# Reordering the latent attention heads of a one-layer block: maxima two items ahead, an earlier shift and row, earlier value products

## The chip, the cores and the metric

The kernel runs on one core of one Trainium2 chip. The metric is the device time of one execution in microseconds (us). The profile is of one profiled execution of the same program; its times count from the start of its span.

## What is computed

The reference is one layer over 1024 latent tokens and 256 context tokens of width 1024, in float32: a half-step SwiGLU, then two token mixers on one normalised input (neighbourhood attention and multi-head latent attention), gated, merged and projected, then a second half-step SwiGLU. The change touches the latent attention: 8 heads, 96 channels for queries and keys (64 plain, 32 rotary), 64 for values; every latent query attends to all 1280 keys.

```python
def _attend(q, k, v):
    s = jnp.einsum('bqhd,bkhd->bhqk', q * q.shape[-1] ** -0.5, k).astype(jnp.float32)
    p = jax.nn.softmax(s, axis=-1).astype(v.dtype)
    return jnp.einsum('bhqk,bkhd->bqhd', p, v)
...
        k_mla = jnp.concatenate([k_ctx_mla, _mla_k(kn, _axial_rope(kr, ang_r, ang_c))], axis=1)
        v_mla = jnp.concatenate([cvb, vb], axis=1)
        o_mla = _blocked_attention(q_mla, k_mla, v_mla)
```

## The kernel before

All matrix products that need float32 accuracy are done as three matmuls of a high and a low part (high x high, high x low, low x high). The layer is a chain of stages: first SwiGLU, projections, neighbourhood attention (`NaItem`, 32 items), latent attention (`MlaItem`, 16 items), merge, second SwiGLU.

A latent item is one head and half of the queries (512); items 2h and 2h+1 belong to head h. The scores are kept with keys on the partitions and queries along the free axis, in ten blocks of 128 keys. These are its steps, with the lines and the names that the profile shows:

- `maxima()` (from L1938): ten steps. Each is a matmul of high parts alone, queries on the partitions, into an `m` bank (bm), and a maximum along it on VectorE (DVE, L1944). The sixteen items have 160 such steps in all; the generator `tops` chains those of all items in order, and each `next(tops)` does one.
- `shift()` (L1963 to L1965): three small DVE operations that turn the maxima into the negated maximum of each query (n_).
- `row()`: a PE transpose of n_ (bm<-ident,st on L160), a DVE copy of it to `kr` (L1972), and four DMAs of 0.5 KB (w<-kr) that write it as row 96 of the head's query tile `qh`. The key tile has ones in that row, so the first score matmul, with 97 rows, subtracts the maximum.
- `scores(kb)`: three matmuls into an `s` bank (bs<-w,w), then the exponential on ScalarE (ACT, L1985). What the text calls block kb is this call with what the loop does behind it.
- `add(kb)`: the sums for the denominator, blocks 0 to 6 on GpSimd (POOL, L1996 and L1998), 7 to 9 on DVE (L2001, L2003); `total()` (L2006) joins both on DVE.
- `weigh()`, the value products: 40 matmuls into a `v` bank (bv<-xp,w) and four of ones with the total (bv<-t,strip) for the denominator.
- `out()`: reciprocal (L2020) and product (L2021) on DVE, a copy on ACT (L1757), and in `heads_out` four output steps on POOL (L1760, L1761).

`MlaHead.first()` issues ten DMAs that load a head's high queries, high keys, context keys and low queries (w<-d); the first four of them bring the high queries and the high latent keys, which the first maximum reads. It also sets the rows of ones with two memsets on POOL. `second()` issues three, for the low keys and the values.

What sets the order of the work: the loop at L2185 calls, for each item and block, `scores`, one or more steps of `tops`, and `follow(i, kb)`, in which the other steps of the preceding item (`prev`), the item itself and the next one (`after`) are written out by block. Matmuls, transposes and DMA issues are pinned to the order of the source (`pin` in L157, L160, L135; all DMAs go through SyncE's queue, SP). DVE, ACT and POOL operations of this stage are not pinned; their order is chosen at build time. Three `m` banks, three `s` banks, two `v` banks, 16 weight tiles `w` and four exponential tiles `xp` (two an item) are shared in turn.

Ahead of the loop the last three neighbourhood items (n = 29, 30, 31) do steps of `tops` in place of scores ahead; the last of them calls `mla_heads[1].first()`, `mla[0].shift()` and, behind its first part, `mla[0].row()`. After the loop `follow(16, kb)` ends the last item, between steps of `FirstMerge` (matmuls bs<-xo,w of the next stage).

Of the kernel before, what the change touches and what calls it, by code (L numbers as in the profile page):

```python
# [22 lines left out]
NH = 8  # L23
# [20 lines left out]
def hybrid_block(ctx: ExitStack, tc: tile.TileContext, a: dict, out: bass.AP):  # L44
# [1230 lines left out]
    def emit_cq(i, ci, x, bank):  # L1275

        t, q = x, T2()
        if bank:
            t = T2()
            act.copy(t, x)  # L1280
        act.activation(q, t, AF.Square)
        if ci in sq:
            vec.tensor_tensor(sq[ci], sq[ci], q, op=ALU.add)
        else:
            sq[ci] = q
        store(cqx[i, :, ci * 512:(ci + 1) * 512], t)
# [22 lines left out]
    for p in range(3):  # L1309
        punits.append(Unit(h2, [cq_src(2 * p), cq_src(2 * p + 1)],  # L1310
                           lambda i, ci, x, bank, p=p: emit_cq(2 * p + i, ci, x, bank)))
# [619 lines left out]
    class MlaItem:  # L1931
# [55 lines left out]
        def part(self, kb):  # L1987
            return self.pt[kb // 5][:, (kb % 5) * 512:(kb % 5) * 512 + 512]
# [39 lines left out]
    soft, started, todo, pending = [], [], [], []  # L2028
    AHEAD, LAG, EARLY = 3, 2, 2

    def start(n):

        if n < len(todo):
            it = todo[n]()
            started.append(it)
            yield from it.scores()
# [79 lines left out]
    tops = chain(*[x.maxima() for x in mla])  # L2116

    def top(n):
        for _ in range(n):
            next(tops, None)  # L2120
            yield
# [3 lines left out]
    def finish_one():  # L2125
        if ending:
            ending.pop(0)()

    for n in range(len(todo)):
        if n == len(todo) - 4:  # L2130
            mla_heads[0].first()
        if n == len(todo) - 2:
            mla_heads[0].second()
        if n == len(todo) - 1:
            mla_heads[1].first()
            mla[0].shift()
        ahead = chain(start(EARLY), start(AHEAD)) if n == 0 else start(n + AHEAD) if n + AHEAD < len(todo) else top(5)
        parts = led_parts[n] if n in led_parts else started[n].values()
        many = len(parts)
        soft_n = list(soft)  # L2140
        for x, part in enumerate(parts):
            pending.append(part() or [])
            take = -(-len(soft_n) // (many - x))
            for f in soft_n[:take]:
                soft.remove(f)
                f()
            del soft_n[:take]
            for _ in range(3 if n == 0 else 1 if n + AHEAD < len(todo) else 2):
                next(ahead, None)
            finish_one()  # L2150
            if len(pending) > LAG:
                ending += pending.pop(0)
                finish_one()
            if n == len(todo) - 1 and x == 0:
                mla[0].row()
        if n == 0:
            next(na1)
        for _ in ahead:
            pass

    def follow(i, kb):


        prev = mla[i - 1] if i else None
        item = mla[i] if i < len(mla) else None
        after = mla[i + 1] if i + 1 < len(mla) else None
        if kb == 0 and prev:
            prev.add(9)
            prev.total()
        if kb == 0 and i % 2 == 0 and i // 2 + 1 < NH:  # L2170
            mla_heads[i // 2 + 1].second()
        if kb == 3 and prev:
            prev.weigh()
        if kb == 4 and prev:
            prev.out()
        if item and kb > 1:
            item.add(kb - 1)
        if after and kb == 5:
            after.shift()
        if kb == 5 and i % 2 and i // 2 + 2 < NH:  # L2180
            mla_heads[i // 2 + 2].first()
        if after and kb == 6:
            after.row()

    for i, item in enumerate(mla):  # L2185
        for kb in range(10):
            item.scores(kb)
            next(tops, None)
            if i == 0:
                finish_one()  # L2190
                if pending and kb % 2 == 0:
                    ending += pending.pop(0)
            follow(i, kb)
            if i >= 14 and kb == 0:
                fm.load(i - 14)
            if i >= 14 and kb == 5:
                fm.split()
    for kb in range(5):
        follow(len(mla), kb)
        for _ in range(3 if kb < 2 else 2):  # L2200
            if fm.left:
                fm.step()
# [264 lines left out]
```

## Time and profile before

| | before |
|---|---|
| median of 3 runs | 2584.81 us (2584.32 to 2588.14) |
| profiled execution | 2584.02 us |
| its span | 2582.2 us |
| PE busy | 2513.7 us (97%) |
| DVE busy | 1853.8 us (72%) |
| ACT busy | 1124.1 us (44%) |
| POOL busy | 301.0 us (12%) |

PE is TensorE. The profile has several views: the page of the whole execution, the waits (who waited for whom, total, times, longest), the instructions in order of time (start, duration, engine, line, operation, output<-input, count, and in brackets the idle time before it and what ended it), the busy time of each engine in stretches (with the granted TensorE clock as a share of full speed), the groups by line, and the DMA issues with the time to landing. L157 is the helper that issues every matmul, L160 every transpose, L135 every DMA, so these are told apart by the tiles that they name. The latent attention lies between 1471 and 1775 us of the span.

### The profile page before, as it was taken

Reading aid. Unit: us, or ns where it says so; the run is one execution under the profiler, and the core shown is the slowest. Engines: PE = TensorE matmul, PEld = TensorE weight load, DVE = VectorE, ACT = ScalarE, POOL = GpSimd, SP = SyncE. Lnnn points to the kernel's source line nnn. Section 1 sums busy time; section 2 is a strip of 40 time slices with the busy share of each in tenths; the row PEclk is TensorE's granted clock in tenths of the full one; section 3 lists DMA queues with packets and bytes.
Section 4 is the critical chain, followed back from the end, with each engine's and each line's share of the span. In section 5 each row is a group of like instructions: output and inputs, shape, how many; then the busy total and the mean of one; then the engine's idle time right before and its main releaser. Section 6 shows DMA issues by size and latency. Waiting matters only on the chain.

```text
span 2582.2 us, 36926 instructions
## 1 busy us (share of the span) xinstructions
PE 2513.7 (97%) x13176; PEld 2080.6 (81%) x13176; DVE 1853.8 (72%) x3162; ACT 1124.1 (44%) x2007; POOL 301.0 (12%) x400
## 2 busy tenths in 40 slices
PE   8999999999999999999999988889999999999998
PEld 6888888888998888889888766667888888888887
DVE  4789986797676588863457666655886888767777
ACT  6623223446654743433538533332267322323444
POOL 1000000001100000001003465553011000000003
PEclk9999999999999999999999999889999999999999
DMA  8555543943674666765857422205846444326824
GB/s 305 164 171 193 190 152 125 342 135 124 236 265 151 236 219 203 261 214 119 285 209 262 126 66 55 62 20 191 315 143 230 151 162 163 115 102 226 280 70 163
DMA packets 247673, 464.74 MB, mean 180 GB/s; under 512 B 61057, under 2 KB 77633, under 8 KB 247489
## 3 DMA queue, kind: packets, MB, share of 16 engines
q1 hardware_dynamic: 247488, 462.38, 53.9%
q8 instruction: 104, 1.70, 0.3%
q14 instruction: 81, 0.66, 0.1%
HBM read 341.59 MB, written 120.65 MB: 179 GB/s over the span
## 4 chain that ended last, share of the span: by engine, by line
PE 90%; DVE 4%; ACT 2%; DMA 2%; issue 1%; SPq 1%; POOL 0%; DVEq 0%; POOLq 0%; ACTq 0%
PE bs L157 38%; PE bm L157 28%; PE bv L157 21%; PE bm L160 2%; DVE t L2020 1%; DVE st L1944 1%; PE bs L160 1%; ACT t L123 1%; SPq L135 1%; DMA w<-kr 1%; DVE xu L123 0%; ACT xu L123 0%; DVE st L1964 0%; ACT xv L123 0%; PE bv L160 0%
## 5 line engine op out<-in xcount | busy, mean ns | idle before, releaser
L123 ACT CAST xu<-t 128x512 fp32r<-128x512 f32 (+1 forms) x270 | 161.0, 601 | 493.7 <-DVE t L123 352.4
L157 PE MATMUL bm<-xu,xu 128*128 128x512 f32 (+2 forms) x1572 | 366.6, 386 | 0.0
L157 PE MATMUL bs<-xv,xu 128*128 128x512 f32 x1488 | 357.4, 389 | 0.3 <-DVE t L123 0.3
L157 PE MATMUL bv<-xv,xu 128*128 128x512 f32 x1342 | 335.4, 389 | 0.0
L157 PEld LDWEIGHTS bm<-xu,xu 128*128 128x128 f32 x1572 | 288.0, 188 | 56.8 <-ACT t L123 0.2
L157 PEld LDWEIGHTS bs<-xv,xu 128*128 128x128 f32 x1488 | 279.1, 188 | 59.0 <-issue 1.1
L157 PEld LDWEIGHTS bv<-xv,xu 128*128 128x128 f32 x1342 | 251.8, 188 | 52.2
L157 PE MATMUL bs<-xv,xv 128*128 128x512 f32 x1086 | 265.9, 390 | 0.0
L123 DVE TENSOR_TENSOR xu<-xu,xu 128x512 fp32r<-128x512 f32 (+1 forms) x296 | 201.8, 686 | 74.4 <-ACT xu L123 74.1
L123 POOL TENSOR_SCALAR st<-st 128x1 f32<-128x1 f32 (+1 forms) x66 | 33.6, 510 | 1882.3 <-ACT t L123 1864.1
L157 PEld LDWEIGHTS bs<-xv,xv 128*128 128x128 f32 x1086 | 203.0, 188 | 41.7
L157 PE MATMUL bs<-w,w 96*128 96x512 f32 (+1 forms) x736 | 210.7, 405 | 16.3 <-DMA w<-kr 13.6
L157 PE MATMUL bs<-xu,xu 128*128 128x512 f32 (+1 forms) x972 | 226.2, 382 | 0.0
L123 DVE TENSOR_TENSOR t<-t,t 128x512 f32<-128x512 f32 (+2 forms) x278 | 185.2, 673 | 45.0 <-ACT t L123 35.9
L157 PEld LDWEIGHTS bs<-xu,xu 128*128 128x128 f32 x972 | 177.4, 188 | 35.7 <-issue 1.4
L123 DVE TENSOR_TENSOR xu<-t,xu 128x512 fp32r<-128x512 f32 (+1 forms) x270 | 179.3, 664 | 10.7 <-ACT xu L123 10.6
L157 PE MATMUL bm<-xv,xv 128*128 128x512 f32 x690 | 182.9, 390 | 0.0
L1985 ACT ACTIVATE xp<-bs 128x512 f32<-128x512 f32 x160 | 95.4, 597 | 193.1 <-PE bs L157 192.7
L123 ACT CAST xv<-t 128x512 fp32r<-128x512 f32 x170 | 105.9, 623 | 166.5 <-PE bv L157 69.2
L157 PEld LDWEIGHTS bs<-w,w 96*128 96x128 f32 (+1 forms) x736 | 132.4, 205 | 45.1 <-issue 16.3
L123 DVE TENSOR_TENSOR xv<-t,xv 128x512 fp32r<-128x512 f32 x170 | 117.0, 688 | 64.9 <-ACT xv L123 64.5
L123 ACT CAST xu<-xu 128x512 fp32r<-128x512 f32 x218 | 132.6, 618 | 68.0 <-DMA xu<-in_wo 38.1
(243 smaller groups left out, 3904.8 us busy)
## 6 DMA issues: line engine op xcount, KB each, us to landing
d<-t SPq DMA_DIRECT2D x366, 256.0 KB, 2.6
t<-d SPq DMA_DIRECT2D x274, 256.0 KB, 3.7
xu<-in_f1w SPq DMA_DIRECT2D x59, 512.0 KB, 4.4
xu<-in_f2w SPq DMA_DIRECT2D x58, 512.0 KB, 3.8
t<-in_wada SPq DMA_DIRECT2D x112, 256.0 KB, 5.1
xv<-in_f1w SPq DMA_DIRECT2D x44, 512.0 KB, 6.5
xu<-in_winT SPq DMA_DIRECT2D x38, 512.0 KB, 4.9
xu<-in_f1w SPq DMA_DIRECT2D x50, 256.0 KB, 5.4
```

Source lines behind the costliest of these rows:

```text
L123: return lambda *x, **y: pin(f(*x, **y))
L135: return pin(nc.sync.dma_start(dst, src))
L157: return pin(nc.tensor.matmul(o, s, m, start=start, stop=stop, skip_group_check=open_group[0]))
L160: return pin(nc.tensor.transpose(o, x, i))
L1944: nc.vector.tensor_reduce(d[:, c:c + pb.shape[-2]], pb, axis=AX.X, op=ALU.max)
L1985: nc.scalar.activation(self.part(kb), pb, AF.Exp)
L2020: nc.vector.reciprocal(rb, pv[:, 256:512])
```

## The change

In the last three neighbourhood items seven steps of `tops` are done instead of five, three a part instead of two, and the row of the first latent item follows the second part instead of the first. In the latent loop block 0 does one maximum, block 1 two, block 2 none and the others one. The value products of the preceding item move from block 3 to block 1, its output from block 4 to block 2, the next item's shift from block 5 to block 1, its row from block 6 to block 3, and the loads of the head after next from block 5 to block 4 of odd items.

```diff
-        ahead = chain(start(EARLY), start(AHEAD)) if n == 0 else start(n + AHEAD) if n + AHEAD < len(todo) else top(5)
+        ahead = chain(start(EARLY), start(AHEAD)) if n == 0 else start(n + AHEAD) if n + AHEAD < len(todo) else top(7)
...
-            for _ in range(3 if n == 0 else 1 if n + AHEAD < len(todo) else 2):
+            for _ in range(3 if n == 0 else 1 if n + AHEAD < len(todo) else 3):
                 next(ahead, None)
...
-            if n == len(todo) - 1 and x == 0:
+            if n == len(todo) - 1 and x == 1:
                 mla[0].row()
...
-        if kb == 3 and prev:
+        if after and kb == 1:
+            after.shift()
+        if kb == 1 and prev:
             prev.weigh()
-        if kb == 4 and prev:
+        if kb == 2 and prev:
             prev.out()
+        if after and kb == 3:
+            after.row()
         if item and kb > 1:
             item.add(kb - 1)
-        if after and kb == 5:
-            after.shift()
-        if kb == 5 and i % 2 and i // 2 + 2 < NH:
+        if kb == 4 and i % 2 and i // 2 + 2 < NH:
             mla_heads[i // 2 + 2].first()
-        if after and kb == 6:
-            after.row()
...
             item.scores(kb)
-            next(tops, None)
+            for _ in range((1, 2, 0)[kb] if kb < 3 else 1):
+                next(tops, None)
```

## Prediction

> **What bounds the kernel now.** I read the profile page first, then the waits of TensorE (PE) in the stage that the change touches, then that stage in order of time.
>
> ```profile
> span 2582.2 us, 36926 instructions
> ...
> PE 90%; DVE 4%; ACT 2%; DMA 2%; issue 1%; SPq 1%; POOL 0%; DVEq 0%; POOLq 0%; ACTq 0%
> ```
>
> PE carries the chain that ended last, so the latent stage is worth what PE loses in it: by waiting, or by running slowly. The stage is from PE's first scores (1471.16) to its last (1764.62). Of its 293.46 us PE is busy 252.12, at a mean granted clock of 0.92 (the column after POOL):
>
> ```profile
> 1471.16:1764.62 293.46, 252.12 (x1372) 181.43 (x1372) 179.95 (x283) 102.16 (x178) 166.16 (x167) 0.92 0.21 52
> ```
>
> The waits of PE there (total, times, longest) add up to 41.4 us:
>
> ```profile
> PE bm L160 <- DVE st L1965: 27.6, 15, 3.0
> PE bs L157 <- DMA w<-kr: 11.8, 8, 3.0
> PE bs L157 <- POOL xo L1761: 1.2, 1, 1.2
> PE bs L157 <- ACT xp L1985: 0.8, 2, 0.4
> ```
>
> The first is the transpose in `row()`, waiting for the negated maxima of `shift()` (L1965); the second the next item's first scores, waiting for the row that `row()` writes by DMA. One item in PE's timeline:
>
> ```profile
> 1610.95 0.27 PE L160 MATMUL bm<-ident,st 128*4 128x128 f32 x1 [1.39 <-DVE st L1965]
> ...
> 1615.23 0.94 PE L157 MATMUL bs<-w,w 97*128 97x512 f32 x3 [1.22 <-DMA w<-kr]
> ...
> 1616.24 0.86 PE L157 MATMUL bs<-w,w 97*128 97x512 f32 x3
> 1616.94 0.39 PE L157 MATMUL bm<-w,w 96*128 96x512 f32 x1
> 1617.17 0.86 PE L157 MATMUL bs<-w,w 97*128 97x512 f32 x3
> ...
> 1619.11 4.54 PE L157 MATMUL bv<-xp,w 128*64 128x256 f32 x40
> 1623.48 0.60 PE L157 MATMUL bv<-t,strip 128*64 128x256 f32 x4
> 1624.01 0.96 PE L157 MATMUL bs<-w,w 97*128 97x512 f32 x3
> ```
>
> From start to start: three score matmuls take 0.70 (1616.24 to 1616.94), the maximum behind them 0.23 (to 1617.17), a block with both 0.93, the value products with their denominator 4.90 (1619.11 to 1624.01). The stage's PE work at this speed is 160 blocks of 0.70 (112.0), 145 maxima of 0.23 (33.4), 15 value products (73.5) and the last neighbourhood product:
>
> ```profile
> 1476.61 2.40 PE L157 MATMUL bv<-t,w 128*64 128x128 f32 x40
> ```
>
> In all 221.3. PE is busy for 252.1; the other 30.8 us are matmuls at half speed. They come in nine spells after waits. Here are the first and the last of the nine, and a whole one, where three scores take 1.49 until 1598.72:
>
> ```profile
> 1473.78 1.49 PE L157 MATMUL bs<-w,w 97*128 97x512 f32 x3
> ...
> 1591.84 0.37 PE L160 MATMUL bm<-ident,st 128*4 128x128 f32 x1 [3.04 <-DVE st L1965]
> 1595.43 1.49 PE L157 MATMUL bs<-w,w 97*128 97x512 f32 x3
> 1598.72 0.86 PE L157 MATMUL bs<-w,w 97*128 97x512 f32 x3
> ...
> 1748.70 5.41 PE L157 MATMUL bs<-w,w 97*128 97x512 f32 x12 [3.03 <-DMA w<-kr]
> ```
>
> So a spell costs 30.8/9 = 3.4 us on average. Waits and spells together, 72 us, are what an ideal order could win.
>
> **The change, part by part.** I count from the start of an item's value products.
>
> *Maxima and shift.* Three more pairs of maxima go ahead of the stage. Item i+1's maxima are then complete before item i begins, and `shift()` is queued on VectorE (DVE) at block 1. Today its three small operations end behind the reciprocal; now they have the 4.9 us of the value products, where DVE idled before (4.02 us in the first row below), ahead of it:
>
> ```profile
> 1624.13 1.76 DVE L2020 RECIPROCAL t<-bv 128x256 f32<-128x256 f32 x1 [4.02 <-PE bv L157]
> 1626.35 0.41 DVE L2021 TENSOR_TENSOR t<-bv,t 128x256 f32<-128x256 f32 x1
> ```
>
> The 27.6 us go to nothing. What is next late there is nothing, as long as the total (L2006) isn't.
>
> *The row.* PE transposes it after block 3, at 4.90 + 0.70 + 0.93 = 6.5. The copy behind it (L1972) is queued on DVE after the reciprocal (5.0 to 6.7), L2021 (to 7.1) and one maximum (0.6): it ends at 7.9, at best at 7.4. The DMAs that follow, on SP's queue, are the four of the row and then:
>
> ```profile
> 1592.56 2.40 SPq L135 DMA_DIRECT2D w<-kr  x4
> 1595.06 5.77 SPq L135 DMA_DIRECT2D w<-d  x10
> 1611.56 2.42 SPq L135 DMA_DIRECT2D w<-kr  x4
> 1614.09 1.63 SPq L135 DMA_DIRECT2D w<-d  x3
> ```
>
> A row's last issue starts 1.8 after its first and lands 1.7 later (row below): at 11.5. The next item's first scores come at 12.1. The 11.8 us of row waits go too, with a cushion of 0.6; for its wear I put 5 us over the stage (0.3 an item, an estimate).
>
> *The next head's loads.* Here I see the price. `first()` is ten DMAs. Before, an odd item i called it at block 5, ahead of its own `row()` (block 6); SP, which issues in source order, reached it right behind the row of item i-1 (1592.56, then 1595.06), about an item and a half before the first maximum that reads it. Now it stands at block 4, behind `row()` at block 3, and is needed sooner: 21 maxima are done when the stage begins, ten more per item, so the last maximum of odd item i is the first of item i+3, a new head. It comes at 6.5 + 5 x 0.93 + 0.70 = 11.9. It needs the first four loads. Their issue waits for the copy (7.9), the row's four (2.4), a gap of 0.1 and three issues of 0.58 (5.77/10), so the fourth starts at 12.2; such loads, early in a group of ten, land 4.0 after issue:
>
> ```profile
> w<-d SPq DMA_DIRECT2D x2, 256.0 KB, 4.0
> ```
>
> ```profile
> w<-kr SPq DMA_DIRECT2D x60, 0.5 KB, 1.7
> ```
>
> They are there at 16.2. PE stands at that maximum, and behind it in PE's order stands the whole next item: a wait of 4.3 us (3.6 with the copy at 7.4), in items 1, 3, 5, 7, 9, 11, for heads 2 to 7. Six waits are 25.8 us. Each wait of 3.0 in the rows above was followed by a spell, so I give each a spell of 3.4: 20.4 us. Bounds: no wait at all, or 6.2 each (the slower rival).
>
> [...]
>
> *Value products two blocks earlier.* The same 44 matmuls. They need the exponentials of the preceding item, long there, and at their end the total. Of GpSimd's (POOL) work an item has these:
>
> ```profile
> L1998 POOL TENSOR_TENSOR t<-t,xp 128x512 f32<-128x512 f32 x79 | 103.8, 1314 | 68.3 <-ACT xp L1985 64.1
> L1761 POOL TENSOR_TENSOR xo<-t,xo 64x256 fp32r<-64x256 f32 x30 | 23.5, 794 | 0.6
> L1760 POOL CAST xo<-t 64x256 fp32r<-64x256 f32 x31 | 12.9, 425 | 0.8
> ```
>
> Six sums and four output steps, 10.3 us. One sum fits beside the value products; from the third exponential (6.2) on, five sums and the output steps run until 15.2, that is 0.9 after the next value products begin; the total follows by 1.6 and is needed at 4.4. Hidden, with 2.8 to spare.
>
> *The start.* Two more maxima in each of the last three neighbourhood items, and the row one part later:
>
> ```profile
> 1458.03 3.26 DVE L1944 TENSOR_REDUCE st<-bm 128x1 f32<-128x512 f32 x5
> ...
> 1466.76 0.27 PE L160 MATMUL bm<-ident,st 128*4 128x128 f32 x1 [0.69 <-DVE st L1965]
> ...
> 1467.26 0.73 PE L157 MATMUL bm<-w,w 96*128 96x512 f32 x2
> ...
> 1471.16 0.94 PE L157 MATMUL bs<-w,w 97*128 97x512 f32 x3 [1.81 <-DMA w<-kr]
> ```
>
> Row to first scores took 4.4. The row now follows the second part's maxima, which ended at 1468.0, plus six maxima of 0.65 on DVE (3.9) less what DVE idles there: first scores between 1.4 (PE's part alone, six of 0.23) and 6 us later. I take 4. The start keeps its spell.
>
> *The end.* After the last block the value products stand behind three merge steps instead of eight; the other merge matmuls follow them. The total was ready at 1769.9, and would be asked for at 1764.6 + 2.1 + 4.4 = 1771.1. Zero; if the total came later, up to 1 us.
>
> ```profile
> 1764.62 5.62 PE L157 MATMUL bs<-xo,w 128*128 128x512 f32 x24
> ...
> 1769.20 0.69 DVE L2006 TENSOR_TENSOR t<-t,t 128x512 f32<-128x512 f32 x1 [2.48 <-POOL t L1998]
> ```
>
> **The sum.** Work 221.3 - 6 x 0.23 = 219.9; head waits 25.8; seven spells of 3.4, 23.8; small waits 5. That is 274.5 against 293.5, 19.0 less; the start takes 4 back: 15. The profiled execution took 2584.02 (span 2582.2 and 1.8 around it), so 2569; the median of the runs lies 0.8 above it: 2570 us.
>
> **The rivals.**
>
> *The loads land in time.* Then six waits and their spells fall out of the sum, 46.2 us: 2524. For it: SP ran far ahead of PE before. Against it: it now has to pass the same item's row, and nothing in the rows shortens copy, issues and landing by more than the 0.5 counted above.
>
> *Short spells.* The shortest spell of the nine is this, from 1629.25 to 1632.92 (the second fence is the chain of work):
>
> ```profile
> 1629.25 1.61 PE L157 MATMUL bs<-w,w 97*128 97x512 f32 x3
> ```
>
> ```profile
> 1632.92 0.71 PE bs L157 x3
> ```
>
> It is 3.7 long and costs 1.8. If all seven were so, 7 x 1.6 = 11 less: 2559. [...]
>
> *The total comes late (slower).* Source order puts the four output steps ahead of an item's sums. If POOL runs them so, the sums begin after the output, at about 10, and end at 17.9, 3.6 into the next value products; the total holds DVE until 4.3, two maxima and the shift until 6.9, and the reciprocal starts 1.9 late. So does the row's copy: the head waits become 6.2 (6 x 1.9 = 11 more) and the row's cushion turns into 1.3 us of wait in the eight other items (10 more): 2591. It decides once the total ends later than about 2.5 after the value products begin. The same follows if the shift ends up behind the reciprocal, so that the change doesn't do what it says. Against both: in the trace the sums that are ready run ahead of the output steps, since the order on DVE and POOL isn't the source's.
>
> **How the numbers follow.** Forecast 0.50 (2558 to 2582: six waits of 3.6 to 5 are 4 either way, the start from 1.4 to 6 some 2.5, small waits from none to 10 another 5), short spells 0.12, loads in time 0.20, late total 0.18. A measurement here tells 0.2%, 5 us, from no change. The upper edge of the forecast and the lower one of the last rival give 0.06 for no change; faster 0.78, slower 0.16. The range reaches down to the middle of the loads-in-time case (half of its 0.20 left out) and up to where the late total begins to show (0.10 left out): 2524 to 2586.
>
> **What would show it.** Right: no wait of L160 for L1965 in the stage; the row landed before the first scores; PE waiting some 4 us for w<-d at the last maximum of items 1 to 11 odd, with 1.49 for three scores after it; even items 14 to 15 us from value products to value products. Wrong: no wait for w<-d at all (then near 2524), or PE waiting in the ones product or for L1972's row in even items (then 2584 and above).

## The result, and the profile after

The changed kernel takes 2574.29 us, the median of 9 runs (2568.87 to 2579.66), against 2584.38 (9 runs, 2583.34 to 2588.14): a ratio of 0.9963 with a 95% interval of 0.9952 to 0.9973, so faster by 0.37%, where the prediction called 0.2% measurable, and 4 us above its figure of 2570. The profiled execution took 2568.87, the shortest of the nine.

Two lines of its page, the span and the chain that ended last; there is a new entry for w<-d:

```profile
span 2567.1 us, 36939 instructions
...
PE bs L157 40%; PE bm L157 28%; PE bv L157 21%; PE bm L160 2%; DMA w<-d 1%; PE bs L160 1%; ACT t L123 1%; DVE xv L123 1%; DVE xu L123 1%; ACT xu L123 0%; DMA xu<-in_f1w 0%; DVE t L123 0%; ACT xp L1842 0%; DVE st L1944 0%; ACT t L1869 0%
```

The waits of PE from 1465 to 1765 (total, times, longest):

```profile
PE bm L157 <- DMA w<-d: 26.5, 6, 5.0
PE bs L157 <- DMA w<-kr: 3.1, 1, 3.1
PE bv L157 <- DVE t L2006: 1.8, 1, 1.8
PE bm L160 <- DVE st L1944: 0.2, 1, 0.2
```

The 27.6 us of L160 waiting for L1965 are gone, and of the row's waits only the first item's is left. In their place stand six waits for w<-d. The stage, from its first scores to its last, in the view of stretches:

```profile
1476.25:1750.28 274.03, 245.71 (x1365) 177.18 (x1365) 197.43 (x274) 101.36 (x178) 168.52 (x167) 0.92 0.23 52
```

274.0 us against 293.5. PE is idle for 28.3 of them instead of 41.3, and busy for 245.7, which is 25.8 above the 219.9 that the prediction counted as its work. Not all of that is half speed, as x7 shows below. The mean granted clock is 0.92 as before. One of the six waits, in order of time:

```profile
1574.86 2.31 SPq L135 DMA_DIRECT2D w<-kr  x3
...
1577.27 7.47 SPq L135 DMA_DIRECT2D w<-d  x13
...
1577.65 0.86 PE L157 MATMUL bs<-w,w 97*128 97x512 f32 x3
...
1583.48 0.77 PE L157 MATMUL bm<-w,w 96*128 96x512 f32 x1 [4.96 <-DMA w<-d]
1584.04 1.48 PE L157 MATMUL bs<-w,w 97*128 97x512 f32 x3
1585.75 1.48 PE L157 MATMUL bs<-w,w 97*128 97x512 f32 x3
```

SP issues the row (the view begins behind the first of its four DMAs), then at 1577.27 the loads of the next head (and, in the same row of the view, the three of `second()`). PE has reached the last block by then; the maximum behind it starts at 1583.48, and the rows of three scores after it are 1.48 long instead of 0.86. The granted clock there is 0.52 (1583.48 to 1587.30), against 1.00 from 1565 to 1578.

### The profile page after: what moved, and what is told of

It reads as the page before. It is cut to its first block, busy times and chain, and to the rows that moved or that the text cites. A ratio compares the mean times of both kernels' runs of the same rounds, so it can differ in the third digit from the quotient of the medians.

```text
span 2567.1 us, 36939 instructions
## 1 busy us (share of the span) xinstructions
PE 2510.4 (98%) x13176; PEld 2078.0 (81%) x13176; DVE 1875.1 (73%) x3162; ACT 1122.9 (44%) x2007; POOL 304.6 (12%) x400
## 4 chain that ended last, share of the span: by engine, by line
PE 91%; DVE 2%; ACT 2%; DMA 2%; issue 1%; POOL 0%; SPq 0%; POOLq 0%; DVEq 0%; ACTq 0%
PE bs L157 40%; PE bm L157 28%; PE bv L157 21%; PE bm L160 2%; DMA w<-d 1%; PE bs L160 1%; ACT t L123 1%; DVE xv L123 1%; DVE xu L123 1%; ACT xu L123 0%; DMA xu<-in_f1w 0%; DVE t L123 0%; ACT xp L1842 0%; DVE st L1944 0%; ACT t L1869 0%
## 5 line engine op out<-in xcount | busy, mean ns | idle before, releaser
L157 PE MATMUL bs<-w,w 96*128 96x512 f32 (+1 forms) x736 | 199.5, 393 | 3.8 <-DMA w<-kr 3.1
```

Source lines behind the costliest of these rows:

```text
L157: return pin(nc.tensor.matmul(o, s, m, start=start, stop=stop, skip_group_check=open_group[0]))
```

## The experiments

Each was timed in five rounds beside the kernel before on the same chip. In x3 extra matmuls are done whose result nobody reads; the other kernels do the same work in another order.

**x1_loads_ahead.** The changed kernel, with the next head's loads ahead of the row.

```diff
+        if kb == 3 and i % 2 and i // 2 + 2 < NH:
+            mla_heads[i // 2 + 2].first()
         if after and kb == 3:
             after.row()
...
-        if kb == 4 and i % 2 and i // 2 + 2 < NH:
-            mla_heads[i // 2 + 2].first()
```

> The changed kernel with one swap: the next head's ten loads are called at block 3 of odd items, ahead of the row, instead of at block 4 behind it. My theory (the loads are late because SP issues them behind the row of the same item): the six waits for w<-d (26.5 us in the changed kernel's profile) go, and with them six half-speed spells of some 3.7 us; the time falls from 2574 by 45 to 50, to about 2527 (2520 to 2535). Rival (the loads are limited by something else, free tiles or the transfers themselves, and only their place in the code differs): waits for w<-d or for w<-kr stay, and the time stays within 2565 to 2576.

Measured: 2530.32 us, ratio 0.9795 (0.9782 to 0.9808), 44 less than the changed kernel. PE's waits of the stage hold no w<-d; the largest are the start's and one for the last total:

```profile
PE bs L157 <- DMA w<-kr: 3.4, 1, 3.4
PE bv L157 <- DVE t L2006: 1.8, 1, 1.8
```

SP's queue shows why. Ten loads again follow a row at once, but it is the row of the item before, and there is time to spare. The fourth load starts near 1493.9 (three issues of 0.6) and, with the 4.0 to landing of the prediction's row, is there at about 1498 (an estimate); the maximum that reads it comes at 1509.11.

```profile
1489.52 2.41 SPq L135 DMA_DIRECT2D w<-kr  x4
1492.03 6.15 SPq L135 DMA_DIRECT2D w<-d  x10
1505.07 2.43 SPq L135 DMA_DIRECT2D w<-kr  x4
```

The order of two calls on one queue was worth four times what the whole change brought.

**x2_loads_later.** The changed kernel, with `kb == 4` of `first()` made `kb == 7`.

> The changed kernel with the next head's loads called at block 7 of odd items instead of block 4, still behind the row. My theory (SP runs ahead of the other engines, so what counts is the place behind the row's copy and not the block): the six waits stay at 4.2 to 5.0 each, and the time at 2574, within 5. Rival (the call's block sets the issue): three blocks of 0.93 later, the waits grow by 2.8 each, 17 in all, to about 2591.

Measured: 2573.92 us, ratio 0.9963 (0.9950 to 0.9977). The sixth wait is put down to DVE's total here, which ended last by the profile; it stands at the same maximum.

```profile
PE bm L157 <- DMA w<-d: 21.6, 5, 4.6
PE bm L157 <- DVE t L2006: 4.7, 1, 4.7
```

26.3 us in six waits, as before: three blocks later in the source change nothing. No other DMA is called between the two places, so the queue's order is the same, and the loads that start at 1577.27 above start at 1577.79 here. SP isn't at the block in which PE is: above, the loads go out 0.10 behind the end of the row's issues (1577.17). The rival falls.

**x3_filled_wait.** The changed kernel, with PE kept at work during the wait.

```diff
         for kb in range(10):
             item.scores(kb)
+            if kb == 9 and i % 2 and i < 12:
+                spare = PB("m")
+                for _ in range(17):
+                    mmul(spare, item.hd.qh[:QK, 0:P], item.hd.kh[:QK, 0:512], True, True)
```

> The changed kernel with 17 extra matmuls ahead of the last maximum of items 1, 3, 5, 7, 9 and 11, whose result nobody reads. They take 17 x 0.22 = 3.7 us, less than the wait of 4.2 to 5.0 that stands there. My theory (idle PE brings the half speed, and it is paid on top of the wait): the waits shrink to 0.5 to 1.2, the spells behind them go, and the time falls by about 6 x 3.7 = 22, to 2552 (2545 to 2558). Rival (the half speed isn't brought by the idle time but by what follows it): the spells stay and so does the time, 2574.

Measured: 2557.39 us, ratio 0.9900 (0.9887 to 0.9914), 16.9 less than the changed kernel. The waits left at that maximum (the profile puts the sixth down to L1965):

```profile
PE bm L157 <- DMA w<-d: 2.4, 5, 0.7
...
PE bm L157 <- DVE st L1965: 0.7, 1, 0.7
```

and one such place, where the scores behind the 17 matmuls run at full speed:

```profile
1573.91 4.02 PE L157 MATMUL bm<-w,w 96*128 96x512 f32 x17
1578.64 0.47 PE L157 MATMUL bm<-w,w 96*128 96x512 f32 x1 [0.71 <-DVE st L1965]
1579.01 0.94 PE L157 MATMUL bs<-w,w 97*128 97x512 f32 x3
1579.79 0.39 PE L157 MATMUL bm<-w,w 96*128 96x512 f32 x1
```

PE stays as long at that place, so what fell is the half speed alone: 16.9 over six is 2.8 us each. I had expected 3.7, which is 25.8 over seven spells, and that took all of the 25.8 for half speed. Useless work made the kernel faster. In the profile of x1 PE is busy for 230.4 us of its stage, 15.3 less than in the changed kernel, which is 2.6 for each of the six:

```profile
1479.65:1712.55 232.90, 230.41 (x1364) 168.57 (x1365) 196.83 (x274) 101.41 (x178) 168.94 (x167) 0.99 0.27 65
```

**x4_values_late.** The changed kernel, with the value products behind the row at block 3 and the output at block 4.

```diff
-        if kb == 1 and prev:
-            prev.weigh()
-        if kb == 2 and prev:
-            prev.out()
         if after and kb == 3:
             after.row()
+        if kb == 3 and prev:
+            prev.weigh()
+        if kb == 4 and prev:
+            prev.out()
```

> The changed kernel with the value products back at block 3 (behind the row) and the output at block 4; maxima, shift, row and loads as changed. My theory (the maxima ahead and the early shift and row free the row; the value products needn't move for it, and between the row and the last maximum they give the loads 4.9 us more): no wait of L160, none for w<-kr, the loads land some 2 us before the last maximum, and the time is about 2528 (2520 to 2538), as with the loads ahead. Rival (the early value products are what frees the row): waits of L160 for L1965 or for w<-kr come back, 1.2 to 3.0 an item with spells, and the time is 2560 or more.

Measured: 2579.67 us, ratio 0.9990 (0.9977 to 1.0003). My theory fell. The loads were in time, as it said (no w<-d among the waits), but the transpose's wait for the shift was back, larger than before:

```profile
PE bm L160 <- DVE st L1965: 36.3, 14, 3.5
```

DVE in one item, with the transpose on PE that waits for it:

```profile
1611.83 1.16 DVE L2006 TENSOR_TENSOR t<-t,t 128x512 f32<-128x512 f32 x1
...
1612.91 0.68 DVE L1944 TENSOR_REDUCE st<-bm 128x1 f32<-128x512 f32 x1
1613.51 0.14 DVE L1963 TENSOR_REDUCE st<-st 128x4 f32<-128x8 f32 x1
1613.69 0.44 DVE L1964 TENSOR_TENSOR st<-st,st 128x4 f32<-128x4 f32 x1
1614.16 0.17 DVE L1965 TENSOR_SCALAR st<-st 128x4 f32<-128x4 f32 x1
...
1614.48 0.27 PE L160 MATMUL bm<-ident,st 128*4 128x128 f32 x1 [2.42 <-DVE st L1965]
```

The reciprocal is nowhere near. The shift waits for its turn behind the total and the maxima, and PE, with two blocks (0.70 and 0.93) after the shift's call, is there first.

**x5_values_only.** The kernel before, with the value products at block 1 and the output at block 2 (`kb == 3` and `kb == 4` made 1 and 2), nothing else.

> The kernel before with one part of the change alone: value products at block 1, output at block 2; maxima one an item ahead, shift at 5, row at 6 and loads as before. Theory A (the reciprocal, queued behind the value products, is what held the shift; moving them two blocks ahead of it frees it): waits of L160 for L1965 fall from 27.6 to under 10, waits for w<-kr stay at 1.2 to 2 an item (the row at block 6 has 2.8 us until the next item's scores and needs 4.4), most half-speed spells go; the time falls by about 40, to 2543 (2533 to 2556). Theory B (the value products only help together with the maxima ahead): waits of L160 stay at 20 or more, and the time at 2565 or more.

Measured: 2585.09 us, ratio 1.0002 (0.9994 to 1.0011). Theory A fell as well:

```profile
PE bm L160 <- DVE st L1965: 32.3, 16, 3.5
PE bs L157 <- DMA w<-kr: 7.0, 6, 1.8
```

The reciprocal is out of the shift's way, and the wait is no smaller: the maxima are complete at block 4, the shift is called at 5 and the row at 6, one block of 0.93 later. So neither the maxima ahead (x4, with the early shift and row) nor the early value products (x5) bring anything alone.

**x8_row_behind_values.** Formed after these two: what counts is the PE work between the call of the shift and the row's transpose. Value products as in x4, but the row behind them, and the loads ahead of the row.

```diff
+        if kb == 3 and prev:
+            prev.weigh()
+        if kb == 3 and i % 2 and i // 2 + 2 < NH:
+            mla_heads[i // 2 + 2].first()
         if after and kb == 3:
             after.row()
+        if kb == 4 and prev:
+            prev.out()
```

> Maxima, shift and start as in the changed kernel; value products back at block 3 and output at block 4; the row at block 3 but behind the value products; the next head's loads at block 3, ahead of the row. Theory C (what counts is how much PE work lies between the call of the shift and the row's transpose, since DVE needs some 3 to 5 us there: the 1.4 us with the value products behind the row was too little, 1.4 and 4.9 are enough, and whether the value products are early or late is nothing in itself): waits of L160 for L1965 under 3 us in all instead of 36.3; the row, copied behind the reciprocal, lands just at the next item's first scores, with waits for w<-kr from none to 0.5 an item; 2532 (2527 to 2542). Theory D (the value products have to be ahead of blocks 2 and 3, for instance so that the reciprocal and the output clear DVE early): waits of L160 or w<-kr of 1 us and more an item, 2560 or more.

Measured: 2530.24 us, ratio 0.9790 (0.9777 to 0.9804), the same as x1. No wait for L1965 is left, and of the row's 4.5 us 3.4 are the start's:

```profile
PE bs L157 <- DMA w<-kr: 4.5, 2, 3.4
PE bs L157 <- ACT xp L1985: 1.3, 3, 0.5
```

Theory C holds, D falls. The loads stand elsewhere than in x4 too, but x4 had no wait for them. With the maxima ahead the value products may stand at block 1 or 3, if they stand between the shift and the row.

**x6_row_first_part** and **x7_row_at_start.** x1 with the start mended: in x6 the first item's row follows the first part again (`x == 1` made `x == 0`), in x7 it stands right behind `mla[0].shift()`, ahead of all parts.

> The changed kernel with the loads ahead of the row, and the first latent item's row back behind the first part of the last neighbourhood item. My theory (the start's 3.4 us of wait for w<-kr is the row being one part late): the wait falls by about 2, the half-speed spell behind it may go; 2530 becomes 2526 (2522 to 2529). Rival (the maxima on DVE set the start): no change, 2530.

> The changed kernel with the loads ahead of the row, and the first latent item's row right behind its shift, ahead of all parts of the last neighbourhood item. My theory: the row has landed before the first scores, the 3.4 us of wait go and the spell of about 3 behind them; 2530 becomes 2524 (2521 to 2527). Rival (the maxima on DVE set the start, or the transposes wait for the shift instead): 2529 or more.

Measured: 2526.37 us, ratio 0.9777 (0.9764 to 0.9790), and 2523.65, ratio 0.9767 (0.9754 to 0.9780). The waits for w<-kr, in x6, and all the waits of 0.2 and more that x7 has left:

```profile
PE bs L157 <- DMA w<-kr: 1.3, 1, 1.3
```

```profile
PE bv L157 <- DVE t L2006: 1.8, 1, 1.8
PE bm L157 <- DVE st L1944: 0.2, 1, 0.2
```

x7 is the best of all, 60 us under the kernel before on the same chip (2583.57).

## Why the prediction held, step by step

- **Bound.** PE's waits and half speed in the stage were the thing to win: x7, which has almost none of either (2.0 us of waits, a granted clock of 1.00 in the stage), is 2.3% faster with the same work.
- **The shift.** Right: no wait for L1965. But its cover is thinner than I had it. I put the total at 1.6 after the value products begin, 2.8 ahead of its use. In the item whose value products begin at 1602.46:

```profile
1601.93 1.27 POOL L1998 TENSOR_TENSOR t<-t,xp 128x512 f32<-128x512 f32 x1
...
1602.49 2.48 DVE L2003 TENSOR_TENSOR t<-t,xp 128x512 f32<-128x512 f32 x1
1603.16 1.26 POOL L1996 TENSOR_TENSOR t<-xp 128x512 f32<-128x512 f32 x1
...
1605.50 0.68 DVE L2006 TENSOR_TENSOR t<-t,t 128x512 f32<-128x512 f32 x1
...
1606.83 0.60 PE L157 MATMUL bv<-t,strip 128*64 128x256 f32 x4
1606.88 0.17 DVE L1965 TENSOR_SCALAR st<-st 128x4 f32<-128x4 f32 x1
...
1607.48 1.76 DVE L2020 RECIPROCAL t<-bv 128x256 f32<-128x256 f32 x1 [0.43 <-PE bv L157]
```

  The total ends at 1606.18, 3.7 after the start and 0.65 ahead of its use; the shift ends 0.43 ahead of the reciprocal's turn. L2003 took 2.48, against 0.68 in the kernel before at 1597.98 with POOL idle, and ended after two of POOL's sums that ran beside it. No run here took POOL's sums away, so why it took longer is not shown. The rival "the total comes late" was nearer than its numbers said. x4 shows what happens when the cover is gone, at another place: 36.3 us.
- **The row.** Predicted copy end 7.9 after the value products begin; with those at 1587.66, the row below ends at 1595.71, 8.05 after. No wait for w<-kr but the first.

```profile
1587.66 4.54 PE L157 MATMUL bv<-xp,w 128*64 128x256 f32 x40
...
1595.44 0.27 DVE L1972 COPY kr<-bm 4x128 f32<-4x128 f32 x1
```

- **The next head's loads.** Six waits of 4.3, 25.8 in all, predicted; six, 26.5 in all, measured, at the places named. x1 and x2 show that the queue's order is the cause, and the rival "the loads land in time" (2524) is what x1 does on purpose (2530).
- **The work and the spells.** Here two terms of the sum were mis-sized and nearly cancelled. The prediction counted 219.9 us of work and put all busy time above its count down to half speed. x7 does the same matmuls in the stage at a granted clock of 1.00, and PE is busy for 227.3:

```profile
1474.74:1703.98 229.24, 227.33 (x1365) 166.50 (x1365) 198.59 (x279) 101.36 (x178) 168.33 (x167) 1.00 0.27 66
```

  So the work was counted 7.4 too low. In x1 an item takes 14.5 to 14.8 from value products to value products (1541.16 to 1555.68, 1497.00 to 1511.83), where ten blocks of 0.93 and 4.90 make 14.2. Of the changed kernel's 245.7 us then 18.4 are half speed, over seven spells 2.6 each, where the prediction had 3.4 and 23.8; x3 gave 2.8, and x1 2.6. By the same count (227.3 and six maxima of 0.23) the nine spells of the kernel before are 2.6 each too. The shortest-spell rival (1.8) is too low for the average.

  The spells are also the likely reason why the runs of this kernel differ by 11 us: their mean granted clock goes from 0.985 to 0.989 as their times go from 2579.66 to 2568.87, while those of x1, without the six, differ by 1.8 (2529.34 to 2531.15). Only the profiled run has a trace, so this stays open.
- **The start** cost 5.1 (1471.16 to 1476.25), within the 1.4 to 6 and above the 4 taken; **the small waits** came to 1.8, not 5, in one place near the end where the ones product waits for the total (one of the signs of being wrong, once only); **the end** to nothing:

```profile
1757.62 6.42 PE L157 MATMUL bs<-xo,w 128*128 128x512 f32 x27
1763.88 2.88 PE L157 MATMUL bm<-xo,xu 128*128 128x512 f32 x12
```

  Before, the next stage's first matmuls came at 1778.54, now at 1763.88 without a gap: 14.7 us, against the 15 of the sum.
- **The time.** For the profiled execution the sum gave 2569 (2568.87 measured). The mechanism was right, but so close a figure is luck: the work was 7.4 too low and the head waits 0.7, the spells 5.4 too high and the small waits 3.2, which leaves 0.5 in the stage. The step to the median was off without a balance: I took 0.8 from the runs of before; it is 5.4, most likely because of the spells.

My theories on what in the change frees the row failed twice, in x4 and x5. The prediction named the 4.9 us of value products between shift and row; it didn't see that neither they nor the maxima ahead do anything alone.

## What to carry to other kernels

Whoever moves a step moves its DMAs. Here all of them go through one queue in the order of the source, and ten loads behind a row that waited for its copy made PE wait for 26.5 us; called ahead of that row they brought no wait, and 44 us less (x1). So put loads that depend on nothing ahead of a small transfer that waits for the compute engines, and count from the queue's place, not from the block of the call (three blocks later: 26.3 us of waits, x2). For a value that goes from one engine through a second and back to the first, count how much independent work the first has between the call that starts it and the one that uses it: with two blocks (1.63 us) PE waited for the shift for 36.3 us in all (x4), with the 4.90 of the value products besides for none (x8); moving one end alone brought nothing here. And in this kernel a wait of some 4 us on TensorE cost 2.6 to 2.8 more behind it, in matmuls at half speed.

## What the runs showed of the hardware that was not expected

- Seventeen matmuls that nobody needs, in a wait of 4 to 5 us, made the kernel 16.9 us faster in six places (x3); the granted clock over the span was 0.997 against 0.989.
- A DVE addition of 128x512 (L2003) took 0.68 us with GpSimd idle (the kernel before, at 1597.98) and 2.48 beside two GpSimd sums (the changed kernel, at 1602.49).
